# One layer of a hybrid SSD and stick-breaking transformer on one core: a written order for scan stage and attention, long and short attention blocks in turn

## The chip, the cores and the metric

The kernel runs on one core of a Trainium2 chip. Its time is the device time of one execution in microseconds (us); lower is better. TensorE is called PE (PEld is its weight load), VectorE DVE, ScalarE ACT, GpSimd POOL, and SyncE, which issues every DMA here, SP. PSUM, into which PE writes, has eight banks of 128 x 512 float32.

## The reference

One decoder layer on 1040 tokens (16 learned meta tokens and 1024 real ones), width 1024, float32. Cut to what matters here:

```python
xn = rms_norm(h, mix_pre_g)
proj = xn @ w_in                        # z, xbc, dt, q, k, v
y_ssd = ssd_mixer(z, xbc, dt, ...)      # scan over 9 chunks: one of 16 tokens, eight of 128; 16 heads in 2 groups
# stick-breaking attention, 16 heads of 64, strictly causal (s < t):
zlog = q @ k.T / 8
beta = sigmoid(zlog); keep = 1 - beta
w[t, s] = beta[t, s] * prod(keep[t, s + 1:t])
y_sb = rms_norm(w @ v)
h = h + rms_norm(concat(y_ssd, y_sb) @ w_out)
h = h + rms_norm(w_down(gelu(dwconv3(xn2 @ w_g)) * (xn2 @ w_u)))
```

## The kernel before

The layer is one long program in stages that keep PE fed. Matmuls with large weights take each operand as a high and a low part (three products for one). The stages, with their times in the profiled execution: norms, projections and convolutions of the SSD part with the first four pairs of heads of q and k, then the values v (all up to 459 us); the **scan stage** (459 to 623 us); **attention** (its loop from 623 to 997 us, its tail to about 1030 us); the output projection and the feed-forward part (to the end). The change touches the scan stage and attention, and one load ahead of them.

**Fill.** Two kinds of work depend on nothing in these two stages and are cut into steps of six matmuls which a Python generator hands out between other work: the projections of q and k for the last four pairs of heads (`qk_fill`, 8 blocks of 16 steps, matmuls of up to 260 columns at L217), and then, for `do`, the halo rows (9 steps) and the first half of the output projection (`mo`, L1329). A quarter of a q or k block (4 steps) fills one PSUM bank; it is emptied by `ev`: ACT copies the high part to `st` (L888), DVE subtracts it from the bank for the low part (L889), and SP stores both. In the scan stage the fill has two such banks, in attention one.

**Scan stage.** 18 units (9 chunks for each of the 2 groups). `chunk_weights` builds the decay matrix `em` of the unit ahead (ACT: 8 relus and an exp from a broadcast load `bc`; PE: `cb`; DVE and POOL: multiply). `chunk_outputs` makes `yf` (PE, from the state), scales it to `yt` (DVE L1003) and renews the state. `chunk_store` sums em times x (PE L1029, 8 matmuls), adds `yt` by four transposing matmuls (L1032), gates it, stores it and squares it for the norm. 80 of the 128 qk fill steps lie in this stage. Nothing here is in a written order: a scheduler with a cost model of its own placed the instructions of each engine and of SP.

**Attention.** For each of 8 pairs of heads `p` and each block `i` of 128 queries (64 steps, `i` from 0 to 7 in turn), `block_weights` computes the logits of all 16 + 128 (i + 1) keys in one to three chunks (PE `z`, L1137), two sigmoids of each chunk (ACT `bt` L1138, `kp` L1142), masks the block's diagonal (POOL L1140), and, once all chunks are there, runs one reversed scan over all keys for each of the two heads (DVE L1144). `block_turn` transposes the weights of the block three steps back, four key blocks in a piece (`tw`, L1157), and ACT copies each piece out (`th`, L1159). `block_mix` multiplies with v one step later, after the first logits (`av`, L1172; ACT copies to `ysc`, L1175). `z` and `tw` share three PSUM tiles of two banks (`zz`); `av` and the fill have one bank each. Once a head pair the 16 meta keys' part follows (`edge_turn`, `edge_mix`: `twc`, `thc`, `avc`, a sum on DVE into `ysc`, L1195, its square `sqb` on ACT, L1202). Only PE's order is written here; the scheduler places the rest.

Of the kernel before, what the change touches and what calls it, by code (L numbers as in the profile page):

```python
# [17 lines left out]
P = 128  # L18
# [20 lines left out]
SCAN_FILL = 36  # L39
OUT_FILL = 14  # L40
FILL_AT = (1, 1, 1, 4, 5, 6, 6, 6)
# [24 lines left out]
def tile_layer(ctx: ExitStack, tc: tile.TileContext, x, meta, rows, parts,  # L66
# [770 lines left out]

    for a, n in enumerate(VORDER):
# [15 lines left out]
    for d, u in zip(vcd, (vd, vdp)):  # L854
        nc.sync.dma_start(out=d.rearrange("(t r) c -> t r c", r=NM),
                          in_=u[P:].rearrange("(t r) c -> t r c", r=P)[:, :NM])
# [3 lines left out]
    xo["b12"] = x_tile(xp, "bxh", "b12rh"), x_tile(xp, "bxl", "b12rl")  # L860
    for t, d in zip(xo["b12"], b12d):
        nc.sync.dma_start(out=t.bitcast(F32), in_=d)

# [10 lines left out]
    def block_w(n):  # L874
        if n < len(qk_blocks) and n not in ready:
            w, p = qk_blocks[n]
            ready[n] = load_w((w_q, w_k)[w][p], f"{'qk'[w]}{p}")
        return ready.get(n)

    left = [0]  # L880

    def qk_fill():
        def chain(n, qs):
            which, p = qk_blocks[n]

            def ev(acc, c0, m):
                st = st_pool.tile([P, 2, CQ], F32R, tag="st", name=f"st{which}{p}{c0}")
                nc.scalar.activation(st[:, 0, :m], acc[:, :m], AF.Copy)  # L888
                nc.vector.tensor_tensor(st[:, 1, :m], acc[:, :m], st[:, 0, :m].bitcast(F32), op=ALU.subtract)  # L889
                nc.sync.dma_start(out=qkd[p][which][:, :, c0:c0 + m], in_=st[:, :, :m].bitcast(F32))  # L890

            return plain_steps(block_w(n), ev, f"{'qk'[which]}{p}", 2, M0 * (which == 0), qs)

        for n in range(len(qk_blocks) - 2):
            for i, end in enumerate(chain(n, QC)):
                if i == 1:
                    block_w(n + 1)
                yield end
        for half in range(2):
            for n in (len(qk_blocks) - 2, len(qk_blocks) - 1):  # L900
                for i, end in enumerate(chain(n, QC[2 * half:2 * half + 2])):
                    if i == 1:
                        block_w(n + 1)
# [12 lines left out]
    def load_q(n):  # L916
        if n < 8 * NT:
            p, i = n // NT, n % NT
            qs[n] = qkp.tile([P, 2, P], F32R, tag="q", name=f"q{p}_{i}", bufs=4)
            nc.sync.dma_start(out=qs[n].bitcast(F32), in_=qkd[p][0][:, :, NM + i * P:NM + (i + 1) * P])  # L920
# [16 lines left out]
    block_w(0)  # L937
    with tc.tile_pool(name="ssd", bufs=1, side="right") as sp:
        dtk = sp.tile([P, 5, NT + 1, 16], F32, name="dtk2", tag="dtk")
        nc.sync.dma_start(out=dtk, in_=dtkd)  # L940
        dt, acs, eac, dec, cdec = (dtk[:, k] for k in range(5))
        state, squares = {}, {}
        for g in range(2):
# [3 lines left out]
            nc.sync.dma_start(out=bt, in_=bcd[g][0])  # L947
            nc.sync.dma_start(out=ct, in_=bcd[g][1])
            nc.sync.dma_start(out=bn[:NM, 0], in_=bnd[g][:NM, 0])
            nc.sync.dma_start(out=bn[:, 1:], in_=bnd[g][:, 1:])  # L950
            state[g] = bt, bn, ct

# [7 lines left out]

        def chunk_weights(g, c):
# [5 lines left out]
            xk = sp.tile([P, 512], F32, tag="xk", name=f"xk{nm}", bufs=2)  # L967
            nc.sync.dma_start(out=xk[:nr], in_=xsd[g][c, :nr, :])
# [9 lines left out]
            nc.vector.tensor_tensor(cbm[:nr, :nr], cb[:nr, :nr], tri[:nr, :nr], op=ALU.mult)  # L978
            for eng, a, e in ((nc.vector, 0, 6), (nc.gpsimd, 6, 8)):
                eng.tensor_tensor(em[:nr, a:e, :nr], em[:nr, a:e, :nr],  # L980
                                  cbm[:nr, :nr].unsqueeze(1).to_broadcast([nr, e - a, nr]), op=ALU.mult)
            xdt = sp.tile([P, 8, 64], F32, tag="xdt", name=f"xdt{nm}", bufs=2)
            nc.gpsimd.tensor_tensor(xdt[:nr], xsc, dt[:nr, c, hs].unsqueeze(2).to_broadcast([nr, 8, 64]),
                                    op=ALU.mult)
            return em, xdt

        def chunk_outputs(g, c, em, xdt, prev):
# [6 lines left out]
            zk = sp.tile([P, 4, P], F32, tag="zk", name=f"zk{nm}", bufs=2)  # L994
            nc.sync.dma_start(out=zk[:, :, y0:nr], in_=zd[g][:, :, c0 + y0:c0 + nr].rearrange("b p t -> p b t"))
            xd = sp.tile([P, 4, P], F32, tag="xd", name=f"xd{nm}", bufs=2)
            nc.sync.dma_start(out=xd[:, :, y0:nr], in_=xdd[g][:, :, c0 + y0:c0 + nr].rearrange("b p t -> p b t"))
            yt = None
            if c > 0:
                yf = psum_sd(f"yf{nm}")  # L1000
                mm(yf[:nr], ct[:, c0:c0 + nr], prev, start=True, stop=True)
# [3 lines left out]
            nprev = None  # L1005
            if c < NT:
                xw = sp.tile([P, 8, 64], F32, tag="xw", name=f"xw{nm}")
                nc.gpsimd.tensor_tensor(xw[:nr], xdt[:nr],
                                        dec[:nr, c, hs].unsqueeze(2).to_broadcast([nr, 8, 64]), op=ALU.mult)
                st = psum_sd(f"st{nm}")  # L1010
                mm(st, bn[:nr, c, :], xw[:nr].rearrange("p h d -> p (h d)"), start=True, stop=True)
                nprev = sp.tile([P, 512], F32, tag=f"prev{g}", name=f"pv{nm}", bufs=2)
                if c == 0:
                    nc.vector.tensor_copy(nprev, st)
                else:
                    nc.gpsimd.tensor_tensor(nprev.rearrange("p (h d) -> p h d", d=64),
                                            prev.rearrange("p (h d) -> p h d", d=64),
                                            cdec[:, c, hs].unsqueeze(2).to_broadcast([P, 8, 64]), op=ALU.mult)
# [3 lines left out]
        def chunk_store(g, c, em, xdt, yt, zk, xd):  # L1022
# [16 lines left out]
            if g == 0:  # L1039
                squares[c] = sp.tile([P, 8, P], F32, tag="sqk", name=f"sqk{nm}")  # L1040
            nc.scalar.activation(squares[c][:, 4 * g:4 * g + 4, ts], zk[:, :, ts], AF.Square)
# [1250 lines left out]
```

## Time and profile before

| | us |
|---|---|
| three runs | 1831.61, 1835.30, 1837.14 (median 1835.3) |
| the profiled execution, its time | 1835.05 |
| its span, first to last instruction | 1833.0 |
| busy in the span: PE, DVE, ACT, POOL | 1686.3, 1068.7, 843.8, 769.6 |
| granted PE clock, mean of the span | 0.967 |
| scan stage (459.3 to 623.3) | 164.0 |
| attention's loop (623.3 to 997.5) | 374.2 |

PE is busy nearly everywhere in the span except in the scan stage and in attention's loop. Since the same matmuls are run whatever their order, the time there is read as PE's work at full clock, its idle time with what ended it, and what a lower clock stretches.

### The profile page before, as it was taken

Reading aid. Unit: us, or ns where it says so; the run is one execution under the profiler, and the core shown is the slowest. Engines: PE = TensorE matmul, PEld = TensorE weight load, DVE = VectorE, ACT = ScalarE, POOL = GpSimd, SP = SyncE. Lnnn points to the kernel's source line nnn. Section 1 sums busy time; section 2 is a strip of 40 time slices with the busy share of each in tenths; the row PEclk is TensorE's granted clock in tenths of the full one; section 3 lists DMA queues with packets and bytes.
Section 4 is the critical chain, followed back from the end, with each engine's and each line's share of the span. In section 5 each row is a group of like instructions: output and inputs, shape, how many; then the busy total and the mean of one; then the engine's idle time right before and its main releaser. Section 6 shows DMA issues by size and latency. Waiting matters only on the chain.

```text
span 1833.0 us, 29194 instructions
## 1 busy us (share of the span) xinstructions
PE 1686.3 (92%) x11472; PEld 1457.3 (80%) x11472; DVE 1068.7 (58%) x1176; ACT 843.8 (46%) x1370; POOL 769.6 (42%) x614
## 2 busy tenths in 40 slices
PE   5899999999689787887899999999999999999998
PEld 5898999978567666775677777899889999888887
DVE  6745544354277555656454146766666565657777
ACT  6444234231456466767666334443333333334544
POOL 3655656521466422324232121267677777600001
PEclk8999999999799799999999999999999999999999
DMA  5242334334799632435321464323223333187335
GB/s 193 90 139 95 112 116 145 151 131 143 220 286 306 175 105 84 147 98 162 94 89 46 133 217 151 115 81 115 87 87 115 100 102 110 58 283 246 103 98 189
DMA packets 161418, 252.92 MB, mean 138 GB/s; under 512 B 17921, under 2 KB 94377, under 8 KB 159602
## 3 DMA queue, kind: packets, MB, share of 16 engines
q1 hardware_dynamic: 161282, 251.07, 42.2%
q8 instruction: 90, 1.47, 0.3%
q14 instruction: 46, 0.38, 0.1%
HBM read 169.08 MB, written 81.92 MB: 137 GB/s over the span
## 4 chain that ended last, share of the span: by engine, by line
PE 47%; issue 4%; ACT 2%; DVE 1%; POOL 1%; DMA 0%; POOLq 0%; DVEq 0%; ACTq 0%
PE fX L1696 9%; PE dnA L2108 7%; PE mo L1329 6%; PE fY L1696 6%; PE fA L1696 6%; PE dnB L2108 5%; PE av L1172 2%; PE tw L1157 1%; PE z L1137 1%; ACT th L1159 1%; PE g0a L1710 1%; ACT bt L1138 0%; ACT kp L1142 0%; PE g0d L1710 0%; PE g0c L1710 0%
## 5 line engine op out<-in xcount | busy, mean ns | idle before, releaser
L1144 DVE TENSOR_TENSOR_SCAN kp<-kp,bt 128x272 f32<-128x272 f32 (+7 forms) x128 | 183.0, 1474 | 131.0 <-POOL bt L1140 57.4
L181 POOL TENSOR_TENSOR wlo<-wr,whi 128x1024 fp32r<-128x1024 f32 x43 | 99.3, 2317 | 42.3 <-ACT whi L180 42.3
L1159 ACT ACTIVATE th<-tw 128x1024 f32<-128x1024 f32 (+2 forms) x96 | 74.7, 816 | 58.0 <-PE tw L1157 57.5
L1146 POOL COPY cb<-kp 128x32 f32<-128x32 f32 x64 | 19.5, 304 | 191.3 <-DVE kp L1144 162.8
L180 ACT ACTIVATE whi<-wr 128x1024 fp32r<-128x1024 f32 x43 | 45.7, 1063 | 112.2 <-PE fX L1696 68.1
L2145 POOL TENSOR_TENSOR fms<-fms 128x1 f32<-128x1 f32 x8 | 2.3, 288 | 222.3 <-DMA ar<-fda 186.2
L1138 ACT ACTIVATE bt<-z 128x288 f32<-128x288 f32 (+6 forms) x112 | 83.5, 746 | 23.6 <-PE z L1137 20.7
L2030 ACT ACTIVATE dh<-ar 128x512 fp32r<-128x512 f32 x77 | 48.6, 631 | 95.2 <-PE dnB L2108 44.7
L1172 PE MATMUL av<-th,v 128*64 128x128 f32 x1152 | 77.3, 279 | 13.4 <-ACT th L1159 13.1
L1137 PE MATMUL z<-k,q 64*128 64x328 f32 (+8 forms) x672 | 79.0, 358 | 11.0 <-DVE st L889 3.8
L1768 DVE SCALAR_TENSOR_TENSOR ga<-gr,pp,ga 128x1024 f32<-128x1024 f32 x44 | 69.2, 1573 | 34.0 <-ACT ga L1761 33.2
L1172 PEld LDWEIGHTS av<-th,v 128*64 128x64 f32 x1152 | 61.7, 137 | 29.3 <-ACT th L1159 23.0
L1142 ACT ACTIVATE kp<-z 128x288 f32<-128x288 f32 (+6 forms) x112 | 84.4, 754 | 0.0
L2031 DVE TENSOR_TENSOR dl<-ar,dh 128x512 fp32r<-128x512 f32 x77 | 53.2, 691 | 47.5 <-ACT dh L2030 47.5
L1137 PEld LDWEIGHTS z<-k,q 64*128 64x128 f32 x672 | 55.9, 199 | 28.6 <-issue 8.7
L1157 PE MATMUL tw<-ident,kp 128*128 128x128 f32 x576 | 78.2, 283 | 0.0
L1157 PEld LDWEIGHTS tw<-ident,kp 128*128 128x128 f32 x576 | 66.8, 145 | 10.2 <-issue 6.6
L1140 POOL TENSOR_TENSOR bt<-bt,low 128x256 f32<-128x256 f32 x64 | 52.5, 820 | 47.2 <-ACT bt L1138 44.9
L2108 PE MATMUL dnA<-dh 128*128 128x512 f32 x176 | 68.6, 390 | 0.0
L2108 PE MATMUL dnA<-dl,dh 128*128 128x512 f32 x176 | 68.5, 389 | 0.0
L2108 PE MATMUL dnA<-dh,dl 128*128 128x512 f32 x176 | 68.5, 389 | 0.0
L1829 POOL TENSOR_TENSOR al<-wr,ah 128x512 fp32r<-128x512 f32 x20 | 28.6, 1428 | 77.6 <-ACT ah L1828 77.5
(989 smaller groups left out, 6188.5 us busy)
## 6 DMA issues: line engine op xcount, KB each, us to landing
wr<-in_w_up SPq DMA_DIRECT2D x44, 512.0 KB
fds<-ga SPq DMA_DIRECT2D x44, 256.0 KB
b<-in_w_down SPq DMA_DIRECT2D x44, 256.0 KB
ar<-fds SPq DMA_DIRECT2D x44, 256.0 KB
fda<-ga SPq DMA_DIRECT2D x33, 256.0 KB
ar<-fda SPq DMA_DIRECT2D x33, 256.0 KB
k<-qkd SPq DMA_DIRECT2D x8, 1040.0 KB
bc<-acsd SPq DMA_DIRECT2D x16, 512.0 KB
```

What stands on the lines that cost most here:

```text
L181: nc.gpsimd.tensor_tensor(l, raw, h.bitcast(F32), op=ALU.subtract)
L1137: mm(z[:, j, :w], u[h, :], r[h, a:a + w], start=s_ == 0, stop=s_ == 2)
L1138: nc.scalar.activation(bt[:, :, a:a + w], z[:, :, :w], AF.Sigmoid, scale=QSCALE)
L1142: nc.scalar.activation(kp[:, :, a:a + w], z[:, :, :w], AF.Sigmoid, scale=-QSCALE)
L1144: nc.vector.tensor_tensor_scan(kp[:, j][:, ::-1], kp[:, j][:, ::-1], bt[:, j][:, ::-1], 0.0, op0=ALU.mult, op1=ALU.add)
L1157: nc.tensor.transpose(tw[:, j, b, :], bt[:, j, c0:c0 + P], ident)
L1159: copied[0] = nc.scalar.activation(th[:, :, :nb, :], tw[:, :, :nb, :], AF.Copy).ins
L1172: mm(av[halves[j], :], v[:, kb, halves[j]], th[:, j, b, :], start=kb == 0, stop=kb == i)
L1329: recent[0] = mm(acc, u[:, k, :], v[:, cs], start=(k == 0 and j == 0), stop=(k == 7 and j == 2))
L1696: mm(acc[:, c, :nn], u[:, k, :], v[:, k, c0:c0 + nn], start=first and k == 0 and j == 0, stop=k == 3 and j == 2, skip_group_check=not first)
L1768: nc.vector.scalar_tensor_tensor(v, self.g[jj][:, :, i:i + 256], fconv_w[:, j, i:i + 1], v, op0=ALU.mult, op1=ALU.add)
L2108: mm(banks[BANK[n], t], u[:, 0, c], v[:, 1, :], start=(n in (1, 2, 5) and p == 0 and i == 0), stop=(p == NPR - 1 and i == 2), skip_group_c ...
```

## The change

All engines and SP now follow the order in which the code is written, from the start of the scan stage to the end of attention (`manual_schedule` with `ALL`). The rest, part by part:

- The second copy of the activations, `b12`, is loaded two products before the end of the v stage. At the start of the scan stage B and C come in slices of one to two chunks (`load_state`), the first chunk's ahead of the small loads; x, z and the skip term are loaded one or two units ahead.
- In a unit the outputs come first, then the weights of the unit ahead. A portion of fill stands between the eight matmuls of `yt` and the four transposing ones. Squares and their sums come a unit later.
- 104 instead of 80 qk fill steps lie in the scan stage, 24 instead of 48 in attention.
- From the last scan unit on (`via_sbuf`) the fill's bank is emptied by two ACT copies, and POOL subtracts from the second.
- Attention takes its blocks in the order 7, 0, 6, 1, 5, 2, 4, 3, with separate `kp` and `bt` buffers for long ones (4 to 7) and short ones. The turn of the block three steps back comes ahead of the step's logits, the values of the turn a step earlier at the step's end. There are four `th` buffers instead of two.
- The scan runs chunk by chunk, each started from the last column of the chunk before. The mask goes from POOL to DVE, and the second piece of a turned long block is copied by DVE instead of ACT.
- v is loaded and subtracted in pieces over the steps, and w_out is loaded a step ahead of its split.

The diff, cut to its core:

```diff
-SCAN_FILL = 36
+SCAN_FILL = 44
-FILL_AT = (1, 1, 1, 4, 5, 6, 6, 6)
+FILL_AT = (2, 1)
+BLOCKS = (7, 0, 6, 1, 5, 2, 4, 3)
+TURN_LAG = 3
...
+        if n == 5:
+            load_b12()
...
                 nc.scalar.activation(st[:, 0, :m], acc[:, :m], AF.Copy)
-                nc.vector.tensor_tensor(st[:, 1, :m], acc[:, :m], st[:, 0, :m].bitcast(F32), op=ALU.subtract)
+                if via_sbuf[0]:
+                    raw = st_pool.tile([P, CQ], F32, tag="sw", name=f"sw{which}{p}{c0}", bufs=1)
+                    nc.scalar.activation(raw[:, :m], acc[:, :m], AF.Copy)
+                    nc.gpsimd.tensor_tensor(st[:, 1, :m], raw[:, :m], st[:, 0, :m].bitcast(F32), op=ALU.subtract)
+                else:
+                    nc.vector.tensor_tensor(st[:, 1, :m], acc[:, :m], st[:, 0, :m].bitcast(F32), op=ALU.subtract)
...
+    ALL = ORDERED | {mybir.EngineType.SP}
+    scan_order = ExitStack()
+    scan_order.enter_context(tc.manual_schedule(engines=ALL))
...
+        def load_state(a, b):
+            for g in range(2):
+                bt, bn, ct = state[g]
+                cs = slice(NM + (a - 1) * P if a else 0, NM + (b - 1) * P)
+                nc.sync.dma_start(out=bt[:, cs], in_=bcd[g][0][:, cs])
+                nc.sync.dma_start(out=ct[:, cs], in_=bcd[g][1][:, cs])
...
                     mm(tp[halves[j], b, :nr], xdt[:nr, 2 * b + j, :], em[:nr, 2 * b + j, :nr],
                        start=b == 0, stop=c == 0, skip_group_check=True)
+            scan_fill()
+            between()
             for b in range(4 * (c > 0)):
                 mm(tp[:, b, :nr], yt[:nr, 2 * b:2 * b + 2].rearrange("p h d -> p (h d)"), ident[:nr, :nr], start=False, stop=True,
                    is_transpose=True, skip_group_check=True)
...
         for n, (g, c) in enumerate(units):
+            if n in (0, 4, 8):
+                load_state(3 + n // 2, 5 + n // 2)
+            if n + 1 < len(units):
+                load_zx(*units[n + 1])
+            if n + 2 < len(units):
+                load_x(*units[n + 2])
+                load_bc(*units[n + 2])
+            yt, zk, xd, prev[g] = chunk_outputs(g, c, *cur)
             nxt = chunk_weights(*units[n + 1]) if n + 1 < len(units) else None
...
+        big = i > 3
+        size, tag = (L, "b") if big else (NM + NT * P // 2, "s")
+        kpt = ap.tile([P, 2, size], F32, tag="kp" + tag, name=f"kp{nm}", bufs=2)
+        btt = ap.tile([P, 2, size], F32, tag="bt" + tag, name=f"bt{nm}", bufs=1 + big)
...
             if ci == 0:
-                nc.gpsimd.tensor_tensor(bt[:, :, n - P:n], bt[:, :, n - P:n],
+                nc.vector.tensor_tensor(bt[:, :, n - P:n], bt[:, :, n - P:n],
                                         low.unsqueeze(1).to_broadcast([P, 2, P]), op=ALU.mult)
             nc.scalar.activation(kp[:, :, a:a + w], z[:, :, :w], AF.Sigmoid, scale=-QSCALE)
-        for j in range(2):
-            nc.vector.tensor_tensor_scan(kp[:, j][:, ::-1], kp[:, j][:, ::-1], bt[:, j][:, ::-1], 0.0,
-                                         op0=ALU.mult, op1=ALU.add)
+            for j in range(2):
+                part = kp[:, j, a:a + w][:, ::-1]
+                nc.vector.tensor_tensor_scan(part, part, bt[:, j, a:a + w][:, ::-1],
+                                             0.0 if ci == 0 else kp[:, j, a + w:a + w + 1],
+                                             op0=ALU.mult, op1=ALU.add)
...
-            copied[0] = nc.scalar.activation(th[:, :, :nb, :], tw[:, :, :nb, :], AF.Copy).ins
+            if u:
+                nc.vector.tensor_copy(th[:, :, :nb, :], tw[:, :, :nb, :])
+            else:
+                copied[0] = nc.scalar.activation(th[:, :, :nb, :], tw[:, :, :nb, :], AF.Copy).ins
...
+        due = mix[:1]
+        if len(turn) >= TURN_LAG:
+            run(begin_turn())
         block = block_weights(p, i)
...
         some(9)
+        for d in due:
+            mix.remove(d)
+            block_mix(*d)
```

What this makes of the order is shown at three places. First PE in a unit of the scan (chunk 3; `pj_` is fill, of which one row stands for six or more like it). Before:

```order
L1001 MATMUL yf_3_5075<-pv_2_4915,ct_4449 128x512
L1011 MATMUL st_3_5081<-xw_3_5079,bn_4450 128x512
L217 MATMUL pj_q_0_0_5064<-b11h,wh_q_4751 128x246
L1029 MATMUL yt_3_5098<-em_3_4960,xdt_3_4976 64x128 x8
L1032 MATMUL yt_3_5098<-ident,yt_3_5077 128x128 x4
L217 MATMUL pj_q_0_0_5064<-b21h,wh_q_4751 128x246
L976 MATMUL cb_4_5144<-ct_4449,bt_4448 128x128
```

In the changed kernel:

```order
L1057 MATMUL yf_3_5184<-pv_2_4921,ct_4451 128x512
L1063 MATMUL st_3_5188<-xw_3_5113,bn_4452 128x512
L1022 MATMUL cb_3_5201<-ct_4454,bt_4453 128x128
L219 MATMUL pj_q_1_260_5169<-b12rh,whi_qk_4777 128x260
L1079 MATMUL yt_3_5218<-em_3_5097,xdt_3_5111 64x128 x8
L219 MATMUL pj_q_1_260_5169<-b22h,whi_qk_4777 128x260
L1084 MATMUL yt_3_5218<-ident,yt_3_5186 128x128 x4
L219 MATMUL pj_k_0_0_5253<-b11h,whi_qk_5078 128x260
```

The transposing matmuls, which read DVE's `yt`, now come behind a portion of fill, and `cb` of the next unit ahead of it.

Second DVE in attention's loop (the rows on `kp` are the scans, with two or more of a kind in a row marked x2, x4). Before:

```order
L1144 SCALAR_TENSOR_TENSOR kp_3_7130<-kp_3_7130,bt_3_7131 128x528 x2
L1195 TENSOR_TENSOR ysc_6725<-avc_7172,ysc_6725 128x8x32
L889 TENSOR_TENSOR st_7192<-pj_q_0_260_6923,st_7192 128x260
L1144 SCALAR_TENSOR_TENSOR kp_4_7203<-kp_4_7203,bt_4_7204 128x656 x2
L1144 SCALAR_TENSOR_TENSOR kp_5_7264<-kp_5_7264,bt_5_7265 128x784 x2
L889 TENSOR_TENSOR st_7306<-pj_k_0_0_7232,st_7306 128x260
```

In the changed kernel:

```order
L1231 SCALAR_TENSOR_TENSOR kp_7_6783<-kp_7_6783,bt_7_6784 128x344 x2
L1231 SCALAR_TENSOR_TENSOR kp_7_6783<-kp_7_6783,bt_7_6784 128x348 x4
L1248 COPY th_4_1_6857<-tw_4_1_6854 128x2x128
L1226 TENSOR_TENSOR bt_0_6860<-bt_0_6860,low 128x2x128
L1231 SCALAR_TENSOR_TENSOR kp_0_6859<-kp_0_6859,bt_0_6860 128x144 x2
L1226 TENSOR_TENSOR bt_6_6906<-bt_6_6906,low 128x2x128
L1231 SCALAR_TENSOR_TENSOR kp_6_6905<-kp_6_6905,bt_6_6906 128x456 x4
L1248 COPY th_7_1_6971<-tw_7_1_6962 128x1024
```

The fill's `st` is gone from DVE; masks, more and shorter scans, and the copy of the second turned piece have come, the copy between the scans of the long block and those of the short one.

Third SP at the start of the scan stage. Before:

```order
L940 DMA dtk_4446<-dtkd 128x720
L947 DMA bt_4448<-bcd_529 128x1040
L948 DMA ct_4449<-bcd_530 128x1040
L949 DMA bn_4450<-bnd_533 16x128
L950 DMA bn_4450<-bnd_533 128x1024
L958 DMA bc_0_4462<-acsd 16x8x16
L890 DMA qkd_543<-st_4497 256x1x246
L968 DMA xk_0_4501<-xsd_116 16x512
```

In the changed kernel:

```order
L978 DMA bt_4450<-bcd_529 128x144
L979 DMA ct_4451<-bcd_530 128x144
L981 DMA bn_4452<-bnd_533 16x128
L982 DMA bn_4452<-bnd_533 128x128
L989 DMA bc_0_4464<-acsd 16x8x16
L1117 DMA dtk_4449<-dtkd 128x720
L997 DMA xk_0_4467<-xsd_116 16x512
L978 DMA bt_4450<-bcd_529 128x128
```

The rows for the second group, which read alike, are left out in both. The first chunks' slices, `bc` and x come ahead, and the rest of B and C in slices behind them.

More of the change, by code (lines that the diff above doesn't have):

```diff
@@ L836, in v_tail, with load_b12 @@
                 nc.sync.dma_start(out=vd[r0:r0 + 8, 256 * c:256 * c + 256], in_=vt_[32 * c + o:32 * c + o + 8])
+    def load_b12():
+        xo["b12"] = x_tile(xp, "bxh", "b12rh"), x_tile(xp, "bxl", "b12rl")
+        for t, d in zip(xo["b12"], b12d):
+            nc.sync.dma_start(out=t.bitcast(F32), in_=d)
     for a, n in enumerate(VORDER):
```

292 lines of the change are left out of this document (167 added, 125 removed).

## The prediction

> **What bounds the kernel now.** I read the busy time by stretches first: the scan stage, attention's loop, a dense stretch, and one stall.
>
> ```profile
> core 0: us, PE busy (x) PEld busy (x) DVE busy (x) ACT busy (x) POOL busy (x), PEclk, DMA share, GB/s
> 459.30:623.30 164.00, 127.96 (x934) 102.48 (x932) 95.97 (x135) 82.70 (x207) 87.05 (x74) 0.89 0.81 255
> 623.30:997.50 374.20, 321.44 (x2866) 256.44 (x2867) 210.18 (x201) 254.29 (x424) 124.53 (x165) 0.93 0.37 109
> 540.00:560.00 20.00, 20.00 (x164) 16.20 (x166) 15.79 (x21) 13.56 (x34) 12.39 (x12) 1.00 0.96 315
> 648.00:656.00 8.00, 3.20 (x37) 2.51 (x35) 5.69 (x8) 4.73 (x9) 3.38 (x3) 1.00 0.27 60
> 656.00:664.00 8.00, 5.49 (x28) 4.89 (x29) 2.45 (x3) 1.32 (x2) 0.90 (x2) 0.57 0.10 33
> ```
>
> In the scan stage PE idles 164.0 - 128.0 = 36 us, in the loop 374.2 - 321.4 = 53 us, and what it does runs at a mean clock of 0.89 and 0.93: 0.11 x 128 = 14 us and 0.07 x 321 = 22 us more are lost to that. No other engine is near its span, so these 125 us are what a better order can win. Next, who PE waits for in the loop:
>
> ```profile
> PE pj_k L217 <- DVE st L889: 13.5, 4, 7.3
> PE av L1172 <- ACT th L1159: 11.9, 22, 3.0
> PE pj_q L217 <- DVE st L889: 11.6, 3, 7.0
> PE halo L1292 <- DVE st L889: 4.7, 1, 4.7
> PE z L1137 <- DVE st L889: 3.8, 1, 3.8
> PE z L1137 <- ACT th L1159: 3.2, 9, 0.7
> ```
>
> The fill's single bank, emptied by DVE's `st`, costs 13.5 + 11.6 + 4.7 + 3.8 = 33.6 us; `th` costs 15.1. The timeline of DVE and PE shows one such wait:
>
> ```profile
> 654.13 4.01 DVE L1144 TENSOR_TENSOR_SCAN kp<-kp,bt 128x912 f32<-128x912 f32 x2
> 658.05 0.40 DVE L889 TENSOR_TENSOR st<-pj_k,st 128x260 fp32r<-128x260 f32 x1
> 658.51 0.58 PE L217 MATMUL pj_k<-b12rh,wh_k 128*128 128x260 f32 x1 [7.27 <-DVE st L889]
> ```
>
> A 0.40 us subtraction stands behind scans, PE stops for 7.27 us, and in the next stretch the clock is 0.57. In the scan stage:
>
> ```profile
> PE yt L1032 <- DVE yt L1003: 15.6, 7, 6.3
> PE cb L976 <- DMA bn<-bnd: 6.0, 1, 6.0
> PE st L1011 <- POOL xw L1008: 5.0, 3, 4.2
> PE cb L976 <- DMA ct<-bcd: 4.0, 1, 4.0
> ```
>
> ```profile
> L1003 DVE TENSOR_TENSOR yt<-yf,dtk 128x512 f32<-128x512 f32 x16 | 10.9, 680 | 4.4 <-PE yf L1001 4.4
> ```
>
> Half is the start, where the first unit's data come behind 3 MB of B and C; half is the transposing matmuls, which stand right behind work that doesn't cover DVE's `yt`.
>
> **The change: the scan stage.** Four terms. The start (6.0 + 4.0 + 5.0 = 15 us): the first chunk's slices come ahead, and some ten issues and a landing remain, which I take as 5 us; **-10**. The transposing matmuls now stand behind 6 to 12 fill matmuls, 0.7 to 1.4 us by the cadence below, against DVE's 0.68 us; I leave 3 of the 15.6; **-13**. More fill, 24 steps x 6 matmuls:
>
> ```profile
> 702.68 0.28 PE L217 MATMUL pj_q<-b11l,wh_q 128*128 128x246 f32 x1
> 703.84 0.28 PE L217 MATMUL pj_q<-b21h,wl_q 128*128 128x246 f32 x1
> ```
>
> Ten starts lie between these, 0.116 us each: 144 x 0.116 = **+17**. The clock gives back 4 of 14 with the waits gone; **-4**. Sum -10: 164 to 154 us.
>
> The bounds of this sum are set by DMA, which is nearly full here:
>
> ```profile
> DMA packets 36950, 41.83 MB, mean 255 GB/s; under 512 B 6032, under 2 KB 28336, under 8 KB 36665
> ```
>
> The bytes stay about the same: b12's 2 MB and k's second MB leave the stage, six more fill stores and two weights enter. At the dense stretch's 315 GB/s 41.8 MB need 133 us; with 5 us ahead of the first load's landing and 7 behind the last, 145 us (-19) is the floor. On the other side, SP in written order holds each unit's loads behind the store of the unit ahead, which waits for DVE's `zk`. If they land 1.2 us late in each of 16 units, the stage takes 19 us more than my sum, 173 (+9).
>
> **The change: attention's loop.** The 24 fill steps that left take 17 us of PE's work along. PE needs 321 x 0.93 = 299 us at full clock, less 17 is 282. The fill's bank is now freed by ACT alone (two copies of 0.42 us, for six banks where there were twelve): what it waits for is the end of the step's sigmoids, not scans, so nearly all of 33.6 us goes. Values a step later take `th` off PE's path (11.9). What comes late next is DVE, which gets work, from POOL among others:
>
> ```profile
> L888 ACT ACTIVATE st<-pj_k 128x260 fp32r<-128x260 f32 x8 | 3.3, 417 | 2.7 <-PE pj_k L217 2.7
> L1140 POOL TENSOR_TENSOR bt<-bt,low 128x256 f32<-128x256 f32 x64 | 52.5, 820 | 47.2 <-ACT bt L1138 44.9 <-DMA v<-vd 1.8
> L1144 DVE TENSOR_TENSOR_SCAN kp<-kp,bt 128x144 f32<-128x144 f32 x16 | 6.8, 466 | 4.6 <-POOL bt L1140 2.5 <-ACT bt L1138 2.1
> L1144 DVE TENSOR_TENSOR_SCAN kp<-kp,bt 128x528 f32<-128x528 f32 x16 | 19.2, 1240 | 0.9 <-POOL bt L1140 0.9
> L1144 DVE TENSOR_TENSOR_SCAN kp<-kp,bt 128x656 f32<-128x656 f32 x16 | 30.4, 1942 | 27.7 <-POOL bt L1140 14.1 <-ACT mh L1299 5.8 <-issue 3.6
> L1144 DVE TENSOR_TENSOR_SCAN kp<-kp,bt 128x784 f32<-128x784 f32 x16 | 30.9, 1974 | 12.3 <-POOL bt L1140 9.7 <-issue 2.5
> L980 DVE TENSOR_TENSOR em<-em,cbm 128x768 f32<-128x768 f32 x16 | 19.8, 1236 | 1.6 <-ACT em L974 1.6
> L1195 DVE TENSOR_TENSOR ysc<-avc,ysc 128x256 f32<-128x256 f32 x7 | 2.8, 397 | 0.0
> L1014 DVE COPY pv<-st 128x512 f32<-128x512 f32 x2 | 1.3, 673 | 0.0
> L889 DVE TENSOR_TENSOR st<-pj_k,st 128x260 fp32r<-128x260 f32 x8 | 3.2, 402 | 0.0
> ```
>
> The rows of 144 and 528 columns give a scan (1240 - 466) / 384 = 2.02 ns a column and 0.18 us a piece. By chunks there are 224 (two for each of 112 chunks) instead of 128: 96 x 0.18 = +17 us. The masks: a third of L980 is 0.41, L1195 has 0.40; 64 x 0.41 = +26. The second pieces have 256, 512, 768 or 1024 columns, eight of each; at 673/512 = 1.31 ns a column, 2560 x 8 x 1.31 = +27. `st` goes: 12 x 0.402 = -5. So DVE's 210 become 275 us, the new bound beside PE's 282.
>
> The rows of 656 and 784 columns lie 0.44 and 0.21 us above that line; I keep them in, though their excess, 16 x 0.65 = 10 us, may go with POOL's masks. [...]
>
> DVE also waits, by these rows of ACT and PE:
>
> ```profile
> L1138 ACT ACTIVATE bt<-z 128x784 f32<-128x784 f32 x16 | 13.3, 830 | 0.6 <-PE z L1137 0.4
> L1142 ACT ACTIVATE kp<-z 128x784 f32<-128x784 f32 x16 | 13.4, 836 | 0.0
> 710.53 0.75 PE L1137 MATMUL z<-k,q 64*128 64x348 f32 x6
> L1202 ACT ACTIVATE sqb<-ysc 128x1024 f32<-128x1024 f32 x6 | 6.4, 1059 | 14.5 <-DVE ysc L1195 14.5
> ```
>
> With three `zz` tiles, the first logits of a long block need the tile that DVE's copy of the second piece frees, and that copy stands behind the scans of the long block ahead. From there `z` 0.75, `bt` 0.83, `kp` 0.84 and three handovers of some 0.15: 2.9 us, which DVE covers with the short block's mask and scans, 1.3, 1.8, 2.4 and 3.2 us for blocks 0 to 3. It waits 1.6, 1.1, 0.5 and 0, some 3 us a head pair, 25 in all. `sqb` waits on ACT for DVE's `ysc` and holds the next `bt` back by 1.06 us and a handover or two: 2 us x 7 = 14. Filling and leaving the loop, 8. So 275 + 47 = **322 us, -52**. The bounds: 285, if all of this is covered (PE's 282 and 3 to fill it), and 460, if nothing is (the first rival). ACT falls by the copies that move, POOL by 52 us of masks; neither comes near. Loads of v, w_out and q have a step or more of slack in a stage whose DMA share is 0.37. The tail and all else run the same matmuls: nothing.
>
> Sum: 1835.05 (profiled; its span is 1833.0, the median of the runs 1835.3) - 10 - 52 = **1773 us**.
>
> **Rivals.**
>
> *Slower: the three engines hand each other each block.* If PE and ACT get no step ahead of DVE, each of two blocks in a pair pays the 2.9 us, and the loop takes 32 x (275/32 + 5.8) = 460 us: 1835 - 10 + 86 = 1911. It decides from waits of (374 + 10 - 275) / 32 = 3.4 us of DVE a pair of blocks, against my 47/32 = 1.5. For it speaks that three tiles are shared by logits and turns and that written queues can't pass a waiting row; against it, that the copy stands ahead of the short block's scans, so only one chain a pair meets it. 0.12.
>
> *All is covered.* Loop 285, scan stage 145: 1835 - 89 - 19 = 1727. For it: scans start chunk by chunk, a long block's first while its last logits are made. 0.10.
>
> *Half of it.* DMA takes the scan stage to 173, and the loop loses only the 33.6 us of `st` and half its clock loss, 11: 1835 + 9 - 45 = 1799. For it: the DMA share of 0.96. 0.16.
>
> *The clock stays down.* If PE's waits, though shorter, keep the clock at 0.75 (between 0.57 behind a stall and 1.00), its 282 us take 376, and the loop gains nothing: 1825. Against it: the waits that are left should be like those on `th`, 11.9 us in 22, or 0.5 us each, far from 7.27. 0.06. [...]
>
> **How the numbers follow.** My forecast gets 0.56, with -62 give or take 25 us. The range leaves out the slower rival and the low half of the covered one: 1735 to 1825. About 0.3%, 5.5 us, is what a measurement can tell from no change. Faster: 0.56 + 0.10 + 0.16 and half of the clock's, 0.85; same: its other half, 0.03; slower: 0.12.
>
> **What would show it.** Right: in the loop no PE wait on `st`, a clock near 1.0, DVE busy for 265 to 280 us and PE waits that end on DVE's copy or its scans; loop about 322, scan stage about 154 with the waits on `yt`, `bn` and `ct` gone. Wrong: a scan stage over 165 with waits on `bc`, `xk` or `zk`, or DVE waiting over 3 us a pair on `bt`, with `z` in turn waiting on the copy `th`.

## The result and the profile after

| | before | after |
|---|---|---|
| median, us | 1835.43 (1831.61 to 1837.14) | 1803.43 (1800.37 to 1806.76) |
| profiled span, us | 1833.0 | 1801.2 |
| scan stage, us | 163.6 | 172.7 |
| attention's loop, us | 373.4 | 340.6 |
| all behind the loop, us | 836.3 | 831.8 |

The ratio is 0.9829, with a 95% interval of 0.9805 to 0.9852: faster by 1.7%, or 32 us where 62 were forecast. One execution each of early, sp_free and the kernel before, in the measurements further down, ran at a mean PE clock of 0.56 to 0.73 and took 17 to 51% longer; medians and ratios leave them out. From here on the stages are cut at the end of the v stage's last product, at the first logits of attention and at the end of the last logits, in every kernel alike; that moves before's two stages by under 1 us against the windows of the prediction. Of the difference in span, 31.8 us, the loop gives 32.8 and what lies behind it 4.5, the scan stage costs 9.1; the other 3.6 lie ahead of the scan stage, whose start varies between 451.6 and 465.5 us among kernels with the same code there.

First the busy time by stretches, the scan stage and the loop of the changed kernel:

```profile
core 0: us, PE busy (x) PEld busy (x) DVE busy (x) ACT busy (x) POOL busy (x), PEclk, DMA share, GB/s
456.10:628.80 172.70, 146.10 (x1078) 120.55 (x1077) 87.52 (x137) 84.54 (x216) 88.37 (x82) 0.94 0.79 240
628.80:969.40 340.60, 308.76 (x2761) 237.10 (x2761) 278.17 (x378) 237.39 (x389) 96.78 (x107) 0.94 0.40 118
```

In each row a busy time is followed by the number of instructions. In the scan stage PE has more to do (1078 matmuls where there were 934) and idles less (27 us where it was 36); DMA carries the same bytes at 240 GB/s instead of 255. In the loop DVE is busy for 278 us, 68 more than before, and PE for some 12 less; the clock is 0.94 there, where nearly 1 was expected.

PE's waits in the scan stage (a row gives the time in all, the number of waits and the longest one):

```profile
PE yt L1079 <- DVE xd L1088: 12.9, 7, 4.3
PE yt L1084 <- DVE yt L1059: 4.0, 4, 1.9
PE st L1063 <- POOL xw L1031: 3.3, 3, 1.6
```

The start's waits on `bn` and `ct` are gone, and 15.6 us on `yt` have become 4.0. New are 12.9 us in which the eight matmuls of `yt` wait for the PSUM tile that DVE's `xd` of the unit before must free. DVE is late because ACT's `em` is: in DVE's order `xd` stands behind the fill's subtraction, which waits for ACT's copy `st`, and that copy stands behind `em`. The waits of ACT, then of SP's queue, in the same stretch:

```profile
ACT em L1018 <- DMA bc<-acsd: 61.9, 14, 11.6
```

```profile
SPq L910 <- DVE st L909: 36.2, 13, 6.3
SPq L1090 <- DVE zk L1089: 18.9, 12, 2.7
SPq L1090 <- DVE st L909: 11.9, 3, 4.9
```

ACT waits 61.9 us for `bc` (16.4 us in 5 waits before the change), and SP's queue stands at its stores, longest at the fill's (L910), behind which the loads of the next units are written. POOL is held up by another of these loads: it waits 29.9 us in 12 waits for `xk`, the unit's x (9.7 us in 4 before). In the chain of work that ended last, followed back through this stage, `xk`, from its issue to its landing, has 22.8% of the time and `bc` 8.1%. One unit in the timelines of SP and ACT:

```profile
541.55 0.33 SPq L1090 DMA_DIRECT2D yd<-zk  x1
541.93 0.43 SPq L1005 DMA_DIRECT2D zk<-zd  x1
542.41 0.56 SPq L1005 DMA_DIRECT2D xd<-xdd  x1
543.07 0.96 SPq L997 DMA_DIRECT2D xk<-xsd  x1
544.07 0.43 SPq L989 DMA_DIRECT2D bc<-acsd  x1
```

```profile
534.53 2.45 ACT L1018 ACTIVATE em<-bc,dtk 128x128 f32<-128x128 f32 x8 [2.15 <-DMA bc<-acsd]
...
549.12 2.45 ACT L1018 ACTIVATE em<-bc,dtk 128x128 f32<-128x128 f32 x8 [2.50 <-DMA bc<-acsd]
```

`bc` is issued at 544.07, last behind the store and three other loads, and ACT, which could have begun at 549.12 - 2.50 = 546.62, gets it at 549.12. Of the two buffers, the one it fills was last read two units earlier, by the `em` that ended at 534.53 + 2.45 = 536.98: it had been free for 7 us.

In the loop, PE's waits and DVE's:

```profile
PE tw L1245 <- DVE th L1248: 7.7, 6, 2.6
PE z L1223 <- DVE th L1248: 7.1, 5, 2.8
PE tw L1245 <- ACT th L1250: 3.8, 6, 1.5
PE z L1223 <- ACT th L1250: 3.6, 4, 2.4
PE pj_k L219 <- ACT sw L906: 3.3, 1, 3.3
```

```profile
DVE bt L1226 <- ACT bt L1224: 32.4, 22, 3.2
DVE kp L1231 <- ACT kp L1228: 6.4, 19, 0.5
```

PE waits on `st` no more, which was 33.6 us; the ACT copy `sw`, which frees the fill's bank now, costs it 4.1 us. It waits 14.8 us for the copy `th` that the change gave to DVE. And DVE, the engine that was to be the bound, is idle for 62 us, more than half of them waiting for ACT's sigmoids.

### The profile page after: what moved, and what is told of

Read it like the earlier page. It is cut to its first block, busy times and chain, and to the rows that moved or that the text cites. A ratio compares the mean times of both kernels' runs of the same rounds, so it can differ in the third digit from the quotient of the medians.

```text
span 1801.2 us, 29222 instructions
## 1 busy us (share of the span) xinstructions
PE 1688.5 (94%) x11472; PEld 1453.4 (81%) x11472; DVE 1127.0 (63%) x1360; ACT 826.7 (46%) x1342; POOL 743.5 (41%) x566
## 4 chain that ended last, share of the span: by engine, by line
PE 64%; DVE 14%; issue 8%; DMA 5%; ACT 4%; POOL 2%; SPq 2%; DVEq 0%; POOLq 0%; ACTq 0%
PE fX L1796 9%; PE dnA L2208 7%; PE fY L1796 6%; PE fA L1796 6%; PE mo L1417 6%; PE dnB L2208 5%; DVE kp L1231 5%; DMA xk<-xsd 2%; PE dXqk L309 2%; DVE cdX L498 2%; PE vB L801 2%; PE z L1223 2%; PE tw L1245 2%; PE av L1262 2%; PE dXx L309 1%
## 5 line engine op out<-in xcount | busy, mean ns | idle before, releaser
L1231 DVE TENSOR_TENSOR_SCAN kp<-kp,bt 128x344 f32<-128x344 f32 (+6 forms) x224 | 198.3, 943 | 12.1 <-ACT kp L1228 6.4
L1234 POOL COPY cb<-kp 128x32 f32<-128x32 f32 x64 | 37.0, 578 | 196.8 <-DVE kp L1231 174.9
L1223 PE MATMUL z<-k,q 64*128 64x348 f32 (+8 forms) x672 | 82.7, 368 | 12.9 <-DVE th L1248 7.1
L1224 ACT ACTIVATE bt<-z 128x688 f32<-128x688 f32 (+6 forms) x112 | 83.9, 749 | 17.3 <-PE z L1223 16.8
L1245 PE MATMUL tw<-ident,kp 128*128 128x128 f32 x576 | 78.0, 281 | 11.5 <-DVE th L1248 7.7
L1228 ACT ACTIVATE kp<-z 128x688 f32<-128x688 f32 (+6 forms) x112 | 84.7, 756 | 0.0
L1223 PEld LDWEIGHTS z<-k,q 64*128 64x128 f32 x672 | 57.1, 203 | 32.4 <-issue 9.3
L1262 PEld LDWEIGHTS av<-th,v 128*64 128x64 f32 x1152 | 63.4, 140 | 23.9 <-issue 10.6
L1245 PEld LDWEIGHTS tw<-ident,kp 128*128 128x128 f32 x576 | 63.1, 143 | 21.7 <-DVE th L1248 9.4
L1018 ACT ACTIVATE em<-bc,dtk 128x128 f32<-128x128 f32 (+1 forms) x144 | 42.6, 378 | 67.8 <-DMA bc<-acsd 61.9
L1250 ACT ACTIVATE th<-tw 128x1024 f32<-128x1024 f32 x64 | 55.8, 872 | 30.7 <-PE tw L1245 30.7
```

The costliest lines, as they stand in the source:

```text
L1223: mm(z[:, j, :w], u[h, :], r[h, a:a + w], start=s_ == 0, stop=s_ == 2)
L1224: nc.scalar.activation(bt[:, :, a:a + w], z[:, :, :w], AF.Sigmoid, scale=QSCALE)
L1228: nc.scalar.activation(kp[:, :, a:a + w], z[:, :, :w], AF.Sigmoid, scale=-QSCALE)
L1231: nc.vector.tensor_tensor_scan(part, part, bt[:, j, a:a + w][:, ::-1], 0.0 if ci == 0 else kp[:, j, a + w:a + w + 1], op0=ALU.mult, op1=AL ...
L1245: nc.tensor.transpose(tw[:, j, b, :], bt[:, j, c0:c0 + P], ident)
L1250: copied[0] = nc.scalar.activation(th[:, :, :nb, :], tw[:, :, :nb, :], AF.Copy).ins
```

## The experiments

All start from the changed kernel and are read against its 172.7 and 340.6 us; the ratios are to the kernel before, as that of the changed kernel, 0.9829, is. How far a stage of one profile can be trusted is seen where an experiment left its code alone: the scan stage 171.7 to 175.5 us in six kernels, the loop 335.6 to 342.6 us in four. Two theories were opposed in each stage. **Scan stage:** SP's written order makes loads late (mine), against DMA's rate or the added fill as the bound. **Loop:** DVE's busy time sets it (mine, from the prediction), against the handing over from engine to engine.

### Loads ahead of the stores (early)

```diff
+        load_x(*units[2])
         cur = chunk_weights(*units[0])
+        load_bc(*units[2])
...
-            if n + 2 < len(units):
-                load_x(*units[n + 2])
-                load_bc(*units[n + 2])
             yt, zk, xd, prev[g] = chunk_outputs(g, c, *cur)
             nxt = chunk_weights(*units[n + 1]) if n + 1 < len(units) else None
+            if n + 3 < len(units):
+                load_x(*units[n + 3])
+                load_bc(*units[n + 3])
```

> The x and decay loads of a unit are issued as soon as the unit two ahead of it has used its buffer, in front of the stores of fill and of y instead of behind them; same bytes, same buffers. If the scan stage is long because SP's written order holds loads behind stores (my theory), ACT's waits on bc (61.9 us) fall to under 25, the stage goes from 172.9 to 155 to 162 us and the median from 1803 to about 1790. If DMA's rate or the extra fill bounds the stage (rivals), it stays at 170 to 175 and the median within 3 us of 1803.

Measured: 1778.77 us, ratio 0.9676 (0.9654 to 0.9698). The stretches (scan stage, then loop), and ACT's wait on `bc`:

```profile
460.40:609.30 148.90, 141.20 (x1078) 117.34 (x1076) 91.51 (x137) 85.41 (x216) 89.49 (x81) 0.95 0.91 278
609.30:944.90 335.60, 302.69 (x2761) 232.07 (x2761) 278.20 (x379) 237.09 (x389) 96.40 (x107) 0.96 0.41 120
```

```profile
ACT em L1018 <- DMA bc<-acsd: 7.8, 3, 6.0
```

The stage falls by 23.8 us to 148.9, further than expected, with the same bytes, buffers and matmuls: DMA at 278 GB/s, PE busy for 141 of 149 us, ACT's wait on `bc` 7.8 us. PE's wait on `xd` falls from 12.9 to 0.3 us as well. The place of two loads, x and `bc`, in SP's queue was worth these 24 us; how they share them isn't told apart, as both were moved. Neither DMA's rate nor the fill bounded the changed kernel's stage.

### The decay loads still further ahead (early_b3)

```diff
-            bc = bcs[g, c] = sp.tile([P, 8, P], F32, tag="bc", name=f"bc{g}_{c}", bufs=2)
+            bc = bcs[g, c] = sp.tile([P, 8, P], F32, tag="bc", name=f"bc{g}_{c}", bufs=3)
...
-                load_bc(*units[n + 3])
+            if n + 4 < len(units):
+                load_bc(*units[n + 4])
```

(against the kernel before it, with units 2 and 3 loaded ahead of the loop)

> As the kernel before in this series, and the decay loads (bc, 512 KB each) one more unit ahead, with a third buffer. My theory: if the latency of a load is what costs, this gives 0 to 5 us beyond the earlier issue, so a stage of 152 to 160 us; PE's 146 us of work would then be the next bound. Rival (DMA rate or fill bounds the stage): 170 to 175 us as in the changed kernel.

Measured: 1782.46 us, ratio 0.9695 (0.9664 to 0.9726); scan stage 148.6 us, 0.3 less than with two buffers. The third buffer gains nothing; what is left is PE's work and DMA's rate (PE is busy for 0.94 of the stage, the DMA share is 0.92).

### SP left to the scheduler (sp_free)

```diff
-    scan_order.enter_context(tc.manual_schedule(engines=ALL))
+    scan_order.enter_context(tc.manual_schedule(engines=ORDERED))
```

> SP is left out of the written order of the scan stage, so that the scheduler puts its loads; PE, ACT, DVE and POOL stay in the written order. In the first half of the stage the scheduler puts the loads where the written order has them, from the tenth unit on ahead of one or two stores. My theory: the stage loses 3 to 8 us, 165 to 170 us, the median 1795 to 1800. Rival (DMA rate): 172 to 174 and 1803.

Measured: 1796.44 us, ratio 0.9751 (0.9705 to 0.9796).

```profile
463.90:621.70 157.80, 141.83 (x1077) 117.90 (x1076) 87.42 (x137) 85.40 (x216) 86.97 (x81) 0.96 0.85 261
```

157.8 us, 15 less, twice what I had expected of an order in which loads go ahead of stores only from the tenth unit on. DMA carries 261 GB/s instead of 240. Giving back SP's order alone thus regains 15 of the 24 us.

### 24 fill steps back in the loop (fill32)

```diff
-SCAN_FILL = 44
+SCAN_FILL = 32
```

> 24 fill steps go back from the scan stage to attention's loop, everything else as changed. If the extra fill is what made the scan stage longer (rival), the stage falls by their 17 us to 156; the loop, bound by DVE, takes part of them: +5 to +17, so a median of 1791 to 1803. If late loads pace the stage (my theory), fewer steps leave it at 165 to 172 and the loop gains 10 us or so: 1803 to 1813.

Measured: 1816.84 us, ratio 0.9893 (0.986 to 0.9926), slower than the changed kernel.

```profile
457.90:627.00 169.10, 134.94 (x932) 108.27 (x931) 85.29 (x132) 80.85 (x207) 85.19 (x76) 0.89 0.77 232
627.00:986.20 359.20, 324.58 (x2905) 252.47 (x2905) 279.60 (x379) 244.56 (x403) 105.69 (x117) 0.95 0.40 118
```

The scan stage loses 3.6 us, not 17: paced by its loads (PE is busy for 134.94 of 169.10 us, with DMA at 232 GB/s where early has 278), it had hidden the added fill nearly whole. The loop gains 18.6 us, more than the 10 that I expected there: its PE has no slack under DVE for 17 us of work. That already speaks against DVE as the loop's bound. The median, 1816.84, lies 4 us above the range expected.

### The masks back on POOL (mask_pool)

```diff
-                nc.vector.tensor_tensor(bt[:, :, n - P:n], bt[:, :, n - P:n],
+                nc.gpsimd.tensor_tensor(bt[:, :, n - P:n], bt[:, :, n - P:n],
```

> The masks of attention's diagonal blocks go back to POOL, all else as in the changed kernel (loop 340.6 us, DVE 278.6 busy). If DVE's busy time sets the loop (my theory), the 31.2 us that leave DVE show: 315 to 330 us, median about 1785. If the handing over between engines sets it (rival), POOL's mask (0.82 us before, against DVE's 0.49) and two more handovers lengthen each block's chain: 340 to 365 us, median 1803 to 1828.

Measured: 1829.14 us, ratio 0.9968 (0.9947 to 0.9989). The loop's stretch, and what DVE waits for in it:

```profile
624.90:989.50 364.60, 316.34 (x2761) 242.13 (x2761) 246.90 (x315) 238.62 (x389) 142.80 (x170) 0.91 0.37 111
```

```profile
DVE kp L1231 <- POOL bt L1226: 78.7, 39, 6.3
```

DVE has 31 us less to do and the loop takes 24 us more. My theory failed here: the mask stands in the chain from logits to scan, and DVE waits 78.7 us for it where POOL makes it.

### One scan for a block (whole)

```diff
-            for j in range(2):
-                part = kp[:, j, a:a + w][:, ::-1]
-                nc.vector.tensor_tensor_scan(part, part, bt[:, j, a:a + w][:, ::-1],
-                                             0.0 if ci == 0 else kp[:, j, a + w:a + w + 1],
-                                             op0=ALU.mult, op1=ALU.add)
+        for j in range(2):
+            nc.vector.tensor_tensor_scan(kp[:, j][:, ::-1], kp[:, j][:, ::-1], bt[:, j][:, ::-1], 0.0,
+                                         op0=ALU.mult, op1=ALU.add)
```

> One scan for a block and head again instead of one for each chunk: 96 scans fewer, 15 us less on DVE. My theory (DVE's busy time sets the loop): 326 to 340 us, median about 1793. Rival (handovers): a long block's scans begin only after its last logits, some 2 us later in each of 32 pairs, so 345 to 390 us, median 1808 to 1850.

Measured: 1818.67 us, ratio 0.9902 (0.9876 to 0.9928).

```profile
638.10:988.50 350.40, 308.83 (x2761) 234.35 (x2761) 260.99 (x285) 237.06 (x389) 81.36 (x107) 0.95 0.39 115
```

```profile
DVE kp L1230 <- ACT kp L1228: 50.9, 35, 2.8
```

17 us less on DVE, 10 us more in the loop: handovers again. DVE waits 50.9 us for ACT's `kp` where it waited 6.4. The early start of a long block's scans is worth more than the 96 extra pieces cost.

### The second pieces' copies back on ACT (th_act)

```diff
-            if u:
-                nc.vector.tensor_copy(th[:, :, :nb, :], tw[:, :, :nb, :])
-            else:
+            if True:
                 copied[0] = nc.scalar.activation(th[:, :, :nb, :], tw[:, :, :nb, :], AF.Copy).ins
```

> The copies of the second pieces (th, 25.5 us on DVE) go back to ACT. My theory (DVE's busy time sets the loop): 317 to 332 us, ACT at 265 us still below it, median about 1785. Rival (handovers): the copies stand on ACT ahead of bt and kp, which DVE waits for: 340 to 355 us, median 1803 to 1818.

Measured: 1796.47 us, ratio 0.9783 (0.9759 to 0.9808). The stretch, then PE's waits, then DVE's:

```profile
633.50:960.60 327.10, 301.28 (x2761) 229.70 (x2761) 254.12 (x347) 252.59 (x419) 96.35 (x107) 0.97 0.42 123
```

```profile
PE z L1223 <- ACT th L1248: 6.3, 6, 1.8
PE z L1223 <- ACT kp L1228: 5.8, 11, 0.7
PE tw L1245 <- ACT th L1248: 4.2, 7, 1.5
```

```profile
DVE bt L1226 <- ACT bt L1224: 48.4, 30, 4.3
```

The loop is 13.4 us shorter (in the times of whole runs it is 8, and the two intervals touch). My theory gave this number, so the time alone doesn't part the two theories; the waits speak against its reason: DVE, freed of 24 us, waits 16 us longer for `bt`. What went are PE's 14.8 us of waits for DVE's `th`, in part replaced by ACT's. PE idles for 25.8 instead of 31.8 us, and for the same 2761 matmuls it is busy for 301.3 instead of 308.8 us, at a clock of 0.97 instead of 0.94. This part of the change, with the others in place, costs time.

### The fill's low half on DVE (st_dve)

```diff
-    via_sbuf[0] = 1
+    via_sbuf[0] = 0
...
-            via_sbuf[0] = int(n > 16)
+            via_sbuf[0] = 0
```

> The low half of fill's results is made by DVE out of PSUM again, not by POOL out of a copy; 7 evictions in the loop, 12 before. At the 2.8 us a piece that PE waited before the change (33.6 for 12) this costs 20 us if PE's waits count: 355 to 362 us, median 1818 to 1825 (my forecast's price). If PE has that much slack beside DVE (rival): 341 to 347 us, median 1803 to 1809.

Measured: 1808.75 us, ratio 0.9841 (0.9808 to 0.9874). The loop, and PE's waits on `st`:

```profile
640.60:977.90 337.30, 302.71 (x2761) 231.47 (x2761) 278.28 (x385) 235.13 (x383) 90.69 (x100) 0.96 0.41 119
```

```profile
PE pj_k L219 <- DVE st L909: 6.4, 2, 5.0
PE pj_q L219 <- DVE st L909: 2.9, 1, 2.9
```

337.3 us, no difference. With DVE's subtraction the waits are 9.3 us and not 20, against 4.1 us on `sw`, and none of it shows in the stage. So the largest wait of the loop before, 33.6 us, was for the most part not removed by the part of the change that was made against it: with that part undone, 24 of the 33.6 us stay away.

### The blocks in order again (inorder)

```diff
-BLOCKS = (7, 0, 6, 1, 5, 2, 4, 3)
+BLOCKS = (0, 1, 2, 3, 4, 5, 6, 7)
...
-        big = i > 3
+        big = True
...
-        kpt = ap.tile([P, 2, size], F32, tag="kp" + tag, name=f"kp{nm}", bufs=2)
+        kpt = ap.tile([P, 2, size], F32, tag="kp" + tag, name=f"kp{nm}", bufs=3)
```

> The blocks of a head pair in the order 0 to 7 again, with three full-length kp buffers in place of two long and two short; all else as in the changed kernel (loop 340.6 us, 335.6 to 342.6 where the loop's code was the same). If a short block between two long ones hides the long one's handovers (my theory), four long blocks in a row lay them open: 350 to 375 us, median 1812 to 1838. If order matters little (rival): 335 to 345 us, median about 1803.

Measured: 1842.08 us, ratio 1.0022 (1.0005 to 1.0038): nothing of the gain is left.

```profile
628.20:1000.60 372.40, 314.37 (x2710) 237.97 (x2710) 279.27 (x378) 240.41 (x390) 94.82 (x108) 0.91 0.37 108
```

```profile
PE z L1223 <- DVE th L1248: 30.1, 8, 6.2
```

31.8 us more at the same DVE work. With long blocks next to each other, the logits wait up to 6.2 us for the tile that DVE's copy frees behind a long block's scans. This kernel also has three kp buffers in place of four, and two bt buffers in place of three; no wait of ACT, which fills them, names them.

### The values in the step of the turn (mix_now)

```diff
-        due = mix[:1]
         if len(turn) >= TURN_LAG:
             run(begin_turn())
+        due = mix[:1]
```

(and the same in the loop that empties the queue)

> A block's values are made in the step that turns it, behind that step's logits and fill, not a step later; all else as in the changed kernel. If the step's delay is what took away PE's wait on th (my forecast's 11.9 us), the loop gets 8 to 20 us longer: 349 to 361 us, median 1811 to 1823. Rival: the copies stand ahead of the step's sigmoids and scans, and are done before the logits are: 336 to 345 us, median about 1803.

Measured: 1827.13 us, ratio 0.993 (0.9903 to 0.9956).

```profile
637.40:994.90 357.50, 310.36 (x2769) 238.14 (x2769) 278.16 (x379) 238.83 (x390) 95.19 (x107) 0.94 0.38 113
```

```profile
PE av L1262 <- DVE th L1248: 15.0, 13, 4.2
PE av L1262 <- ACT th L1250: 11.8, 8, 3.0
```

16.9 us more, within what I expected; 26.8 us of waits of `av` on `th` come back, the larger part on the copies that DVE makes, while those of `z` on `th` fall from 10.7 to 6.4 us and no wait of `tw` on `th`, 11.5 us before, is among the seven largest any more (the seventh is 1.6 us).

### Both finds together (early_th, early_th_st)

The first joins the edits of early and th_act, the second adds that of st_dve; the lines that mark them:

```diff
+                load_bc(*units[n + 3])
...
-            if u:
+            if True:
...
-    via_sbuf[0] = 1
+    via_sbuf[0] = 0
```

> The early loads and the copies of the second pieces on ACT in one kernel. If the two are independent (scan stage -23.8 us, loop -13.4 us): scan stage 147 to 151, loop 323 to 331, median 1764 to 1772. Rival: PE, busy for 141 of the one's 149 us and 303 of the other's 327, sets both already and eats part of it: 1772 to 1785.

> As the kernel before in this series, with the low half of fill's results made by DVE out of PSUM in the loop as well. My theory, after it cost nothing in the changed kernel: DVE now has slack and gets 3 us of work, so within 4 us of the same, 1762 to 1772. Rival: with DVE no longer the bound the bank's wait on DVE counts, 5 to 15 us more: 1773 to 1783.

Measured: 1771.01 us, ratio 0.9646 (0.9623 to 0.9669), and 1775.73 us, ratio 0.9662 (0.9634 to 0.9691).

```profile
462.50:611.70 149.20, 141.43 (x1078) 117.28 (x1076) 91.37 (x137) 85.28 (x216) 89.52 (x82) 0.95 0.89 278
611.70:937.50 325.80, 300.93 (x2761) 229.37 (x2761) 254.56 (x347) 252.65 (x419) 96.11 (x107) 0.97 0.42 124
```

The stages add up as expected, 149.2 and 325.8 us: early_th is faster than the kernel before and the changed one, by 65 and 32 us. Against early alone its gain, 5.5 us by the ratios, lies inside the intervals; it is the profile's loop, 325.8 against 335.6 to 342.6, that bears it out. With st_dve's edit added the median lies in the rival's range, not in mine, and the loop was 333.8 us in its profile, while the times of the two can't be told apart; whether the fill's detour over POOL earns anything stays open.

## Why the prediction was right in sign and half off in size

**The scan stage's sum** was where it failed: 154 us forecast, 172.7 measured. Its terms can be found. In the first 32 us PE was busy for 27.4 instead of 17.7 us, the start's -10; the wait on `yt` fell by 11.6, forecast -13; PE's busy time rose by 18.1, where the fill's +17 and the clock's -4 make 13. The step that failed is the adding up itself. It took PE's old list of waits, shortened, as the list that would be left, and put at nothing the waits that late loads would bring. PE idled for 26.6 us instead of 36.0, 9.4 less where 23 were forecast, and the new wait on `xd` alone is 12.9. This is what the prediction had named as its sign of being wrong: a stage over 165 us, with waits on `bc` and `xk`. Nor did this stage, paced by its loads, get shorter by 11.6 us less of waits on `yt`, or much longer by the added fill (fill32: 3.6 us for 24 steps).

The late loads were in the text as the upper bound, 1.2 us in each of 16 units, 173 us, and I gave them the "half of it" rival's 0.16, which called them DMA's rate. The mechanism of the bound was the right one and the name in the rival the wrong one: early and sp_free show it was the queue. Even the bound named only the store that waits for `zk` (18.9 us) and not the fill's, at which the queue stood longer (36.2 us). That 173 was met so closely is luck, as no row gave the 1.2 us. The bound from below, 145 us by bytes over the dense stretch's rate, was near what the same work took when its loads were early, 148.9.

**The loop's terms.** DVE's work was forecast well, 275 against 278 us. Its part as "the new bound" was not, and this is the step that failed here: taking 31 or 17 us off DVE made the loop longer (mask_pool, whole), and when taking 24 off made it 13 shorter (th_act), DVE idled for 10.6 us more. The waits were forecast as 47 us and are 62: the chain from logits to mask, "25 in all", is 32.4 + 6.4 = 39. (A handover, put at 0.15 us without a row, isn't what makes it long: where DVE takes up ACT's result at 704.87, 705.60, 736.61 and 737.32 us, it begins 0.03 to 0.04 us after ACT's end.) In PE's terms, 308.8 us busy at 0.94 are 290 at full clock, not 282, and the stretch now holds 2761 matmuls where 2859 - 144 = 2715 were due; at 0.116 us each the 46 more are 5 of these 8 us. The groups of PE's instructions name them: 27 more of `tw` and 24 more of `av` lie ahead of the last logits (and 5 fewer of the output product), because the block that is left to be turned and mixed behind them is now a short one. In inorder the count is 2710 again. This work is missing behind the loop (4604 matmuls instead of 4650), where 4.5 us are gone that I had put at nothing. 18.5 us are lost to the clock, 32 to idling.

**st.** That PE's wait on `st` would go was right; that the two ACT copies were needed for it was not, as st_dve shows.

**The rivals.** "Half of it", 1799 us, was closest to the measured 1803: its scan stage, 173, is right, and its loop, 45 off, is not far from 32.8 and 4.5 behind it. But the reason that it gave, DMA's rate, is not the one that the runs show. "Hand to hand", 1911, was wrong in its price but right in its kind: DVE's idle time a pair is (340.6 - 278.2)/32 = 1.95 us, between my 1.5 and the 3.4 from which it decides, and inorder, at 372 us, goes a quarter of the way to its 460.

**The 10 us above the line.** The prediction kept this excess of the scans of 656 and 784 columns in and thought that it might go with POOL's masks. No such gain came: over the whole run the scans took 183.3 us before and 199.0 after, 16 more, where the extra pieces alone were put at 17. POOL still subtracts v, and a timeline of POOL and one of DVE show a scan beside it:

```profile
713.71 1.28 POOL L1177 TENSOR_TENSOR v<-v,w 128x512 f32<-128x512 f32 x1 [2.20 <-DMA w<-vcd]
```

```profile
713.76 1.79 DVE L1231 TENSOR_TENSOR_SCAN kp<-kp,bt 128x264 f32<-128x264 f32 x1
```

By the line of 2.02 ns a column that scan takes 0.71 us, and the eight scans of 264 columns that no instruction of POOL overlaps took 0.68 to 0.71; it took 1.79 beside a POOL instruction of 1.28. Of the seven others that v's subtraction overlaps, four took 1.56 to 1.73 us and three 0.71. In the kernel before, none of the scans of 656 and 784 columns overlaps a mask. The twenty that v's subtraction doesn't overlap took 1.49 to 1.52 us (656 columns) and 1.76 to 1.79 (784), and of the twelve that it overlaps nine took 2.07 to 2.87. So the excess came beside v's subtraction and not beside the masks; why some of these scans took longer and others not isn't shown. In all, v's subtraction overlaps DVE's scans for 15.1 us before the change and for 19.3 us in the changed kernel. In mask_pool, with POOL's masks back, the scans in the loop took 182.9 us, 13.4 less than the 196.3 of the changed kernel, and 12.6 of these lie in the scans of 264 and 328 columns (715 instead of 896 ns, 853 instead of 1086).

**What stays open.** Undone one at a time, the parts cost the loop 31.8 (order), 24.0 (masks), 18.6 (fill), 16.9 (values' step) and 9.8 us (scans by chunk), and undoing `th` gains 13.4. That sums to far more than the 32.8 us between the two kernels. So the parts need each other, or the written order costs time that they win back; the values' step, moreover, was not put back to where the kernel before has it. How the 32.8 us are to be shared isn't settled, as no run adds a part alone to the kernel before, and what the written order itself earns in the loop isn't known, as no run gives the loop back to the scheduler.

## What to carry to other kernels

When an order is written for the engine that issues DMAs too, look at what each load stands behind: a store that waits for the end of a chain delays the loads that start the next one, and here two loads moved ahead of it were worth 24 us without a byte or a buffer more. A list of waits on the busiest engine is not a sum of what can be won; ask first what paces the stage, for example by taking work out of it and seeing whether it gets shorter. And where three engines hand work around, an engine's busy time is no bound by itself: work may be moved onto the fullest engine if that shortens the chain (the masks, 24.0 us), and must not be if another engine stands waiting for it (the copies of the second pieces, 13.4 us).

## What the hardware showed unexpectedly

TensorE's clock was at 0.50 behind two short waits, without one long stall like the 7.27 us in the kernel before. Two stretches of the changed kernel's loop, and PE's rows in the first of them:

```profile
741.90:745.30 3.40, 0.83 (x9) 0.29 (x6) 1.03 (x1) 3.40 (x7) 2.74 (x2) 1.00 0.52 154
745.30:752.10 6.80, 6.17 (x38) 3.71 (x40) 6.56 (x9) 5.42 (x9) 2.39 (x2) 0.50 0.66 169
```

```profile
743.25 0.44 PE L1262 MATMUL av<-th,v 128*64 128x128 f32 x4 [1.06 <-ACT ysc L1265]
745.21 1.08 PE L1245 MATMUL tw<-ident,kp 128*128 128x128 f32 x4 [1.51 <-ACT th L1250]
```

Two waits of 1.06 and 1.51 us leave PE busy for 0.83 of 3.40 us, and for the next 6.8 us the clock is 0.50.

The loop has eight stretches at a clock of 0.50, which last 3.4 to 6.8 us and begin at 636.1, 653.1, 677.0, 724.8, 745.3, 758.9, 840.9 and 956.9 us. In the 3.4 us ahead of each PE was busy for 0.61 to 1.55 us, and its longest idle time there was 1.5 to 2.8 us. What starts such a stretch isn't shown by this: in the kernel before, one begins at 632.4 us, and in the 3.40 us ahead of it PE was busy for 3.12.

So my forecast of a clock near 1, on the ground that the waits left would be short, was wrong: 0.94, and in th_act, with 13.4 us less, 0.97.
